# Spreading the root of three RMS norms over the partitions: two transfers through DRAM in place of four products

## The chip, the cores and the metric

The kernel runs on one core of one Trainium2 chip. A core has five engines that work side by side, each through its own queue in its own order: TensorE (PE in the profile; its weight loads are PEld), VectorE (DVE), ScalarE (ACT), GpSimd (POOL) and SyncE (SP), which here only issues transfers (DMAs). The engines share the on-chip memory SBUF (128 partitions); TensorE writes its results to PSUM, which GpSimd does not use here. The metric is the time of one execution on the device in microseconds; lower is better.

## What is computed

One encoder layer, then a final norm, for 1024 prompt tokens and 256 sample tokens of width 1024 with the same weights:

```python
def rmsnorm(x, w):
    y = xf * lax.rsqrt(jnp.mean(xf * xf, -1, keepdims=True) + EPS)
    return (y * w.astype(jnp.float32)).astype(x.dtype)
...
x = x + merged @ w_out
x = x + memory_cross_attention(rmsnorm(x, norm_xa_w), rmsnorm(mem, norm_mem_w), xa_w_q, xa_w_kv, xa_w_o)
h = rmsnorm(x, norm_ffn_w)
gu = h @ ffn_w_gate_up
x = x + (jax.nn.silu(gu[..., :D_FF]) * gu[..., D_FF:]) @ ffn_w_down
...
return rmsnorm(x, final_norm_w)
```

All of it is float32. The change touches the norm before the feed-forward part (`norm_ffn_w`) and the final norm, both for some of the tokens only.

## The kernel before

Activations lie feature-major: a tile is 128 features on the partitions by the tokens along the free axis, and the width of 1024 is eight such tiles (`KT`, index k). Tokens go in three blocks (`BLOCKS`): 0 and 1 are 512 prompt tokens each, 2 is the 256 sample tokens. Every float32 product is done as three products of split operands: a matrix is copied to a high half (`hi`, `whi`, on ScalarE) and the rest is subtracted into a low half (`lo`, `wlo`, on VectorE or GpSimd); `mm3` multiplies hi by hi, hi by lo and lo by hi into one PSUM bank (a tile of 128x512, `bank`). L108 is the line of nearly every product, L125 and L126 are those of the two splits.

The mean square of a token is a sum over features, so over partitions. `Norm.add` squares each of the eight tiles on ScalarE and adds them up in `acc` (named nacc in the profile) on VectorE or GpSimd. `Norm.rest` then does, in this order:

- Products of 128 tokens of `acc` by a column of ones (128x1), one for each of the `nb` = 4 groups of 128 tokens: the sums lie with tokens on the partitions, 128x4.
- On that small tile, `rsqrt` on VectorE (L231 to L235): `y` (nst in the profile), the reciprocal root of the mean square, 128x4.
- The way back to features on the partitions: four products of a column of `y`, broadcast, by the identity. They leave in one bank the root of each of 512 tokens, the same on all partitions.
- Eight multiplications by that root and the weight column, one for each k. Most are one scalar_tensor_tensor on VectorE (L294), which reads the tile from SBUF and the root from the bank. For the k in `shared`, ScalarE multiplies by the weight column ahead of time (L289) and GpSimd by the root (L290), which it reads from a copy in SBUF that ScalarE makes from the bank (L286, into `acc`).
- `sink(k, t)` hands each result on.

Three uses matter here. I call them the first, the second and the third place:

- The first is the feed-forward norm of block 0, in `OutProj.run`: all eight k on VectorE, in place; the sink splits the results into the feed-forward input. It runs while TensorE does the output projection of blocks 1 and 2. Ahead of it SyncE stores the block before the norm to DRAM (`x2d`).
- The second is the final norm of block 1, in `last_norm`, started after phase 5 (of 0 to 6) of the prompt's down projection. k = 1, 3, 5 and 7 are GpSimd's. The sink stores each result to the output `yT`: odd k from SyncE's queue, even k from ScalarE's.
- The third is the final norm of block 0, started after phase 6, so it runs beside the sample's down projection (`down_sample`). k = 1, 4 and 6 are GpSimd's. In `down_sample` each of 22 rows of weights for each half of the width is split by `prep` into one of four buffer pairs (`his`, `los`) while TensorE works on the earlier ones; `prep(n + 4)` follows tile n.

Beside the second and third place the sample's activations come back from DRAM: SyncE loads `graw`, ScalarE and VectorE split it into gs (`g_room`). At the end of phase 6 VectorE evacuates four banks of sums into x (L2241); the sample's down projection uses these banks next.

The order of the work: the body is a main generator with side generators. A planner's clock counts the nominal time of TensorE's products, and a side generator goes on when the clock reaches the time that it last asked for with `yield`. So `lag`, `lag2` and `pace` (in ns of that clock) set where a norm's steps stand in program order. TensorE keeps that order; for the other engines a scheduler orders instructions by what they depend on. Waits are semaphores; an engine that waits holds up what is behind it in its queue.

Of the kernel before, what the change touches and what calls it, by code (L numbers as in the profile page):

```python
# [8 lines left out]
F32 = mybir.dt.float32  # L9
F32R = mybir.dt.float32r  # L10
I32 = mybir.dt.int32
AF = mybir.ActivationFunctionType
ALU = mybir.AluOpType
# [4 lines left out]
P = 128  # L18
D = 1024
KT = D // P  # L20
# [147 lines left out]
def trunk_kernel(ctx: ExitStack, tc: tile.TileContext, a):  # L168
    nc = tc.nc
    V, S, G, T, SY = nc.vector, nc.scalar, nc.gpsimd, nc.tensor, nc.sync  # L170
    K = Trunk(ctx, tc, a)
# [19 lines left out]
    n = 0  # L191
# [25 lines left out]
    ident = cst[:, C_ID : C_ID + P]  # L217
# [6 lines left out]
    def bank(p=pq, tag="b"):  # L224
        return p.tile([P, 512], F32, tag=tag, name="bank")
# [11 lines left out]
    class Norm:  # L237
# [21 lines left out]
                (eng or V).tensor_tensor(out=self.acc, in0=self.acc, in1=sq, op=ALU.add)  # L259
            self.k += 1  # L260

        def rest(self, xk, wcol, sink, pace=1300, shared=(), lag=1500, ks=range(KT), inplace=False, ready=None, halves=1, lag2=2800, rooms=()):

            p, n = self.p, self.n
            nb = n // P
            yield lag
            pc = bank()
            parts = [self.acc[:, i * n : (i + 1) * n] for i in range(halves)]
            if self.apart is not None:
                parts.append(self.apart)  # L270
            for c in range(nb):
                for t in parts:
                    mm(pc[:, c : c + 1], t[:, c * P : (c + 1) * P], one, t is parts[0], t is parts[-1])
            y = p.tile([P, 4 if p is xp else 16], F32, tag="nst", name="nst", bufs=2)[:, :nb]
            ms, sc = pc[:, 4 : 4 + nb], pc[:, 8 : 8 + nb]
            V.tensor_scalar(out=ms, in0=pc[:, :nb], scalar1=1.0 / D, scalar2=EPS, op0=ALU.mult, op1=ALU.add)
            rsqrt(y, ms, sc)
            yield lag2
            pb = bank()
            for c in range(nb):  # L280
                mm(pb[:, c * P : (c + 1) * P], y[:, c : c + 1].to_broadcast([P, P]), ident)
            while ready is not None and not ready():
                yield 300
            if shared:
                rb = self.acc
                S.activation(rb, pb[:, :n], AF.Copy)  # L286
            for k in ks:
                if k in shared:
                    S.activation(xk(k), xk(k), AF.Copy, scale=sm[:, wcol + k : wcol + k + 1])  # L289
                    G.tensor_tensor(out=xk(k), in0=xk(k), in1=rb, op=ALU.mult)  # L290
                    sink(k, xk(k))
                    continue
                t = bank() if k in rooms else xk(k) if shared or inplace else p.tile([P, 512], F32, tag="nsq", name="nt", bufs=self.sq)[:, :n]
                V.scalar_tensor_tensor(out=t, in0=xk(k), scalar=sm[:, wcol + k : wcol + k + 1], in1=pb[:, :n], op0=ALU.mult, op1=ALU.mult)  # L294
                sink(k, t)
                yield pace * n / 512

    def rstd_of(nm, y, lag, lag2=0, halves=1):
        n = nm.n
        nb = n // P  # L300
        yield lag
        pc = bank()
        parts = [nm.acc[:, i * n : (i + 1) * n] for i in range(halves)]
        for c in range(nb):
            for t in parts:
                mm(pc[:, c : c + 1], t[:, c * P : (c + 1) * P], one, t is parts[0], t is parts[-1])
        ms, sc = pc[:, 4 : 4 + nb], pc[:, 8 : 8 + nb]
        V.tensor_scalar(out=ms, in0=pc[:, :nb], scalar1=1.0 / D, scalar2=EPS, op0=ALU.mult, op1=ALU.add)
        rsqrt(y, ms, sc)
        yield lag2  # L310

    def norm(p, xk, n, wcol, sink, pace=1300, step=700, lag=1500):
        nm = Norm(p, n)
# [1131 lines left out]
    class OutProj:  # L1445
# [21 lines left out]
        def run(self, xsrc, scale, wcol, xpool, store, sinks=None, then=None, after=None):  # L1467


            ps = (xpool,) * 3 if sinks is None else (x0p, xhp, xpool)  # L1470
            x = [p.tile([P, KT, n], F32, tag=f"x{b}", name=f"x{b}") for b, (p, (_, n)) in enumerate(zip(ps, BLOCKS))]
            for ks in (slice(0, 2), slice(2, 8)):
                for b, (t0, n) in enumerate(BLOCKS):
                    SY.dma_start(x[b][:, ks, :], xsrc[:, ks, t0 : t0 + n])
            nms = [Norm(xpool, n) for _, n in BLOCKS]

            def evac(m, b, ps):
                V.scalar_tensor_tensor(out=x[b][:, m, :], in0=ps, scalar=scale, in1=x[b][:, m, :], op0=ALU.mult, op1=ALU.add)
                nms[b].add(x[b][:, m, :])

            begun, self.first = self.first, []
            for i, (m, b) in enumerate((m, b) for m in range(2) for b in range(3)):
                if i < len(begun):
                    yield from proj(begun[i], self.ws[m], self.src, b, range(KT - 2, KT))
                    evac(m, b, begun[i])
                else:
                    yield from self.parts(m, b, range(KT))
                    evac(m, b, self.first[-1])
                if (m, b) == (1, 0):
                    K.ahead()  # L1490
            hs = self.hs
            for b, (t0, n) in enumerate(BLOCKS):
                for m in range(2, KT):
                    if b == 0:
                        self.ws.append(K.take())
                    ps = bank(pm)[:, :n]
                    yield from proj(ps, self.ws[m], self.src, b)
                    if b == 0 and m < KT - 1 or b == 2 and m == 6:
                        K.ahead()
                    evac(m, b, ps)  # L1500
                    if b == 2 and after is not None:
                        after(m)
                if b == 0:
                    hs += act_tiles()
                if then is not None and b == 0:
                    then()
                if store is not None:
                    SY.dma_start(store[:, :, t0 : t0 + n], x[b])
                xk = lambda k, b=b: x[b][:, k, :]
                if sinks is None:  # L1510
                    norm_b = nms[b].rest(xk, wcol, to_h(hs, b), 600)
                else:
                    norm_b = nms[b].rest(xk, wcol, sinks(b, hs), PACES[b], ks=range(KT) if b != 1 else SECOND_KS, inplace=True, lag2=LAGS2[b])
                K.pending[id(hs), b] = K.side(norm_b)
            self.x = x

# [759 lines left out]
    def last_norm(nm, b):  # L2276
        t0, n = BLOCKS[b]

        def sink(k, t):
            (SY if k % 2 else S).dma_start(a["yT"][:, k, t0 : t0 + n], t)  # L2280

        if b < 2:
            K.side(nm.rest(lambda k: x2[b][:, k, :], S_FIN, sink, PACEF, SHARED[b], LAGF[b], lag2=LAGF2[b]))
            return
        pb = bank()
        ms, y = pb[:, :n], pb[:, n : 2 * n]
        parts = [nm.acc, *nm.apart]
        for t in parts:
            mm(ms, mean.to_broadcast([P, P]), t, t is nm.acc, t is parts[-1])
        r = x2p.tile([P, 512], F32, tag="nacc", name="seed", bufs=2)[:, :n]  # L2290
        S.activation(r, ms, AF.Abs_reciprocal_sqrt, bias=eps)
        V.scalar_tensor_tensor(out=y, in0=ms, scalar=EPS, in1=r, op0=ALU.add, op1=ALU.mult)
        V.scalar_tensor_tensor(out=y, in0=y, scalar=-0.5, in1=r, op0=ALU.mult, op1=ALU.mult)
        xk = lambda k: x2[b][:, k, :]
        for k in EARLY_K:
            G.tensor_tensor(out=xk(k), in0=xk(k), in1=r, op=ALU.mult)
        root = bank()[:, :n]
        for k in EARLY_K:
            V.scalar_tensor_tensor(out=xk(k), in0=y, scalar=1.5, in1=xk(k), op0=ALU.add, op1=ALU.mult)
            sink(k, xk(k))  # L2300
            if k == EARLY_K[0]:
                V.scalar_tensor_tensor(out=root, in0=y, scalar=1.5, in1=r, op0=ALU.add, op1=ALU.mult)
                S.activation(nm.acc, root, AF.Copy)
                for j in (2, 0):
                    G.tensor_tensor(out=xk(j), in0=xk(j), in1=nm.acc, op=ALU.mult)
        for k in (4, 2, 5, 6, 0, 7):
            if k > 3:
                V.scalar_tensor_tensor(out=xk(k), in0=xk(k), scalar=sm[:, S_FIN + k : S_FIN + k + 1], in1=root, op0=ALU.mult, op1=ALU.mult)
            sink(k, xk(k))
# [95 lines left out]
MIX = 6500  # L2405
A1, A2, A3, A4 = 1200, 800, 2000, 600
DEC, CONV = 1200, 600
FIRST_W, PACES, LAGS2 = 9000, (600, 1300, 600), (2800, 9500, 9500)
LAGX = (26000, 17000, 9000)
FIRST_V = (1, 3, 5, 6, 7)  # L2410
LAG0, LAGF, LAGF2, PACEF = 9700, (8000, 6000, 1500), (9000, 9000, 2800), 1000

SHARED, EARLY_K = ((1, 4, 6), (1, 3, 5, 7)), (1, 3)

# [78 lines left out]
```

## Time and profile before

| | |
|---|---|
| median of 3 runs | 2184.68 us (2183.58 to 2186.11) |
| profiled execution | 2185.21 us |
| its span, first to last instruction | 2183.4 us |
| granted TensorE clock, mean | 0.998 of full speed |
| the root's products on TensorE, all norms | 60 records of 128x128, 275 ns median |
| ScalarE's copies of the root (L286) | 2, 598 ns |
| GpSimd's multiplications by the root (L290) | 7, 1291 ns median |
| VectorE's multiplications by the root (L294), 128x512 | 467 to 749 ns over all shapes |
| transfers | 253.04 MB, mean 116 GB/s |

The span is divided by engine and line; a wait is given as the engine and line that waited, what it waited for, the total, the number of times and the longest. In a timeline a row is one instruction or a run of equal ones: start, duration, engine, line, operation, tile written and tiles read, shapes, count, and in brackets the idle time ahead of it and what ended it. TensorE's matmuls overlap, so their starts tell the pace. DMA rows give the size and the time from issue to landing.

### The profile page before, as it was taken

How to read it: one execution, taken by the hardware profiler on the slowest of the kernel's cores; microseconds unless marked ns; L12 is line 12 of the kernel's file. 1: busy time of each engine (PE TensorE's matmuls, PEld its weight loads, DVE VectorE, ACT ScalarE, POOL GpSimd, SP SyncE). 2: the span in 40 equal slices, each digit the busy share in tenths (PEclk: the TensorE clock that was granted, in tenths of full speed). 3: DMA queues.
4: the chain of work that ended last, by engine and by line, in shares of the span. 5: the costliest groups of instructions: out<-in, count | busy, mean ns of one | idle time of the engine just before them, and what ended most of it. 6: DMA issues, size and time to landing. Idle time of an engine off the chain costs nothing.

```text
span 2183.4 us, 31946 instructions
## 1 busy us (share of the span) xinstructions
PE 2169.1 (99%) x12184; PEld 1888.5 (86%) x12184; DVE 1354.3 (62%) x2615; ACT 885.7 (41%) x1651; POOL 592.8 (27%) x399
## 2 busy tenths in 40 slices
PE   9999999999999999999999999999999999999998
PEld 8988888888888888888988888888888888888888
DVE  7868678786874846677644556544434444478575
ACT  6433263544535553125544523332322323343454
POOL 2010110101001010052412432566666665200031
PEclk9999999999999999999999999999999999999999
DMA  5221423323244546631522421322222222493531
GB/s 195 92 93 54 113 61 95 84 66 93 76 121 123 169 134 225 203 131 55 178 73 108 158 97 63 104 86 84 83 77 80 84 98 90 147 348 119 205 112 59
DMA packets 194297, 253.04 MB, mean 116 GB/s; under 512 B 76933, under 2 KB 109269, under 8 KB 194143
## 3 DMA queue, kind: packets, MB, share of 16 engines
q1 hardware_dynamic: 177886, 227.14, 31.8%
q10 hardware_dynamic: 16256, 23.86, 3.0%
q8 instruction: 95, 1.56, 0.3%
q14 instruction: 60, 0.48, 0.1%
HBM read 178.02 MB, written 72.94 MB: 115 GB/s over the span
## 4 chain that ended last, share of the span: by engine, by line
PE 94%; DVE 3%; DMA 1%; ACT 1%; issue 0%; SPq 0%; POOL 0%; DVEq 0%; ACTq 0%; POOLq 0%
PE bank L108 93%; PE bank L121 1%; DMA braw<-gq 1%; DMA raw<-in_w_sv 0%; DVE gb L819 0%; DVE nt L294 0%; DVE U L948 0%; ACT junk L517 0%; DVE aT L814 0%; DMA gb<-grd 0%; DVE lo L126 0%; DVE bank L294 0%; DMA uc<-usd 0%; DVE gt L491 0%; DVE nacc L259 0%
## 5 line engine op out<-in xcount | busy, mean ns | idle before, releaser
L108 PE MATMUL bank<-hi,whi 128*128 128x512 f32 (+1 forms) x1976 | 700.9, 355 | 0.2 <-DVE vg L493 0.2
L108 PE MATMUL bank<-lo,whi 128*128 128x512 f32 (+1 forms) x1976 | 687.7, 348 | 0.0
L108 PE MATMUL bank<-hi,wlo 128*128 128x512 f32 (+1 forms) x1976 | 687.4, 348 | 0.0
L108 PEld LDWEIGHTS bank<-hi,wlo 128*128 128x128 f32 x1976 | 374.3, 189 | 47.9
L108 PEld LDWEIGHTS bank<-hi,whi 128*128 128x128 f32 x1976 | 375.0, 190 | 45.8 <-issue 1.4
L108 PEld LDWEIGHTS bank<-lo,whi 128*128 128x128 f32 x1976 | 375.1, 190 | 43.2
L125 ACT ACTIVATE whi<-raw 128x1024 fp32r<-128x1024 f32 (+1 forms) x136 | 137.0, 1009 | 249.5 <-PE bank L108 221.5
L126 POOL TENSOR_TENSOR wlo<-raw,whi 128x1024 fp32r<-128x1024 f32 x65 | 158.1, 2433 | 293.9 <-ACT whi L125 293.9
L126 DVE TENSOR_TENSOR wlo<-raw,whi 128x1024 fp32r<-128x1024 f32 (+1 forms) x71 | 80.8, 1140 | 74.6 <-ACT whi L125 74.4
L108 PE MATMUL bank<-bhl,whi 128*128 128x512 f32 x408 | 125.9, 390 | 0.0
L126 POOL TENSOR_TENSOR wlo<-x,whi 128x1024 fp32r<-128x1024 f32 x40 | 96.6, 2414 | 47.5 <-ACT whi L125 47.5
L2123 DVE TENSOR_TENSOR x<-x,bank 128x512 f32<-128x512 f32 x21 | 14.5, 689 | 124.5 <-ACT x L1918 124.5
L108 PEld LDWEIGHTS bank<-bhl,whi 128*128 128x128 f32 x408 | 76.4, 188 | 16.4 <-ACT whi L125 0.4
L697 DVE SCALAR_TENSOR_TENSOR acc<-craw,sm,acc 128x510 f32<-128x510 f32 (+1 forms) x96 | 73.2, 762 | 24.6 <-ACT acc L695 22.8
L1931 DVE SCALAR_TENSOR_TENSOR t<-t,x 128x512 f32<-128x512 f32 x42 | 63.9, 1521 | 28.7 <-ACT t L1930 28.7
L125 ACT ACTIVATE whi<-x 128x1024 fp32r<-128x1024 f32 (+1 forms) x48 | 49.2, 1025 | 77.5 <-PE bank L108 69.6
L108 PE MATMUL bank<-bhl,wlo 128*128 128x512 f32 x204 | 79.6, 390 | 0.5 <-DVE wlo L126 0.5
L1940 DVE SCALAR_TENSOR_TENSOR t<-bank,t 128x512 f32<-128x512 f32 (+1 forms) x44 | 24.5, 557 | 81.4 <-PE bank L108 81.4
L108 PE MATMUL bank<-bhl,ahl 128*128 128x512 f32 x312 | 75.0, 395 | 0.0
L1069 ACT ACTIVATE gs<-bank 128x512 f32<-128x512 f32 (+1 forms) x60 | 31.2, 520 | 101.2 <-PE bank L108 94.2
L1918 ACT ACTIVATE x<-bank 128x512 f32<-128x512 f32 x63 | 37.6, 597 | 82.0 <-PE bank L108 79.3
L108 PEld LDWEIGHTS bank<-bhl,ahl 128*128 128x128 f32 x312 | 58.8, 189 | 13.6
(420 smaller groups left out, 4459.1 us busy)
## 6 DMA issues: line engine op xcount, KB each, us to landing
raw<-in_w_gu SPq DMA_DIRECT2D x44, 512.0 KB, 3.4
braw<-gq SPq DMA_DIRECT2D x14, 1024.0 KB, 7.5
raw<-in_w_g SPq DMA_DIRECT2D x20, 512.0 KB, 3.3
gq<-t SPq DMA_DIRECT2D x33, 256.0 KB, 2.1
gtd<-gs ACTq DMA_DIRECT2D x32, 256.0 KB, 2.2
w<-in_w_dn SPq DMA_DIRECT2D x8, 1024.0 KB, 9.7
raw<-in_w_qkv SPq DMA_DIRECT2D x12, 512.0 KB, 3.6
gq<-r SPq DMA_DIRECT2D x22, 256.0 KB, 2.0
```

Source lines behind the costliest of these rows:

```text
L108: self.nc.tensor.matmul(out, l, r, start=start, stop=stop, skip_group_check=more)
L121: self.nc.tensor.transpose(out, x, ident)
L125: self.last_hi = self.nc.scalar.activation(hi, src, AF.Copy).ins
L126: (eng or self.nc.vector).tensor_tensor(out=lo, in0=src, in1=f32(hi), op=ALU.subtract)
L697: V.scalar_tensor_tensor(out=dst, in0=src, scalar=wj, in1=dst, op0=ALU.mult, op1=ALU.add)
L1069: S.activation(t, ps, AF.Tanh, scale=0.5)
L1918: S.activation(t, ps, AF.Copy)
L1931: V.scalar_tensor_tensor(out=t, in0=t, scalar=1.0, in1=src, op0=ALU.add, op1=ALU.mult)
L1940: V.scalar_tensor_tensor(out=out, in0=u, scalar=sign, in1=t, op0=ALU.mult, op1=ALU.mult)
L2123: V.tensor_tensor(out=c22, in0=c22, in1=pe, op=ALU.add)
```

## The change

In the three places the root no longer goes through TensorE. SyncE writes `y` to a row of a small DRAM tensor, `rows_d` (three rows of 512 floats): each partition writes its four values, 16 bytes, so that token 128 c + p stands at position 4 p + c. A second transfer reads that row, broadcast to all 128 partitions, into `acc`. All multiplications then take the root from `acc` in SBUF, through a view with steps of four elements (16 bytes) that puts the tokens back in order. The copies by ScalarE go. Other norms keep the products.

The planner's lags change too: between the root and the read stand 3500 (`ROW`), after it `lag2`, 7000 at the first place (2800 before) and 6500 at the other two (9000 before).

```diff
-        def rest(self, ..., halves=1, lag2=2800, rooms=()):
+        def rest(self, ..., halves=1, lag2=2800, rooms=(), row=None):
...
             rsqrt(y, ms, sc)
-            yield lag2
-            pb = bank()
-            for c in range(nb):
-                mm(pb[:, c * P : (c + 1) * P], y[:, c : c + 1].to_broadcast([P, P]), ident)
+            if row is not None:
+                SY.dma_start(row.rearrange("(p c) -> p c", c=nb), y)
+                yield ROW
+                SY.dma_start(self.acc, row.unsqueeze(0).to_broadcast([P, n]))
+                yield lag2
+                rb = pb = self.acc.rearrange("q (p c) -> q c p", c=nb)
+            else:
+                yield lag2
+                pb = bank()[:, :n]
+                for c in range(nb):
+                    mm(pb[:, c * P : (c + 1) * P], y[:, c : c + 1].to_broadcast([P, P]), ident)
+                if shared:
+                    rb = self.acc
+                    S.activation(rb, pb, AF.Copy)
             while ready is not None and not ready():
                 yield 300
-            if shared:
-                rb = self.acc
-                S.activation(rb, pb[:, :n], AF.Copy)
+            like = (lambda x: x) if row is None else quad
             for k in ks:
                 if k in shared:
                     S.activation(xk(k), xk(k), AF.Copy, scale=sm[:, wcol + k : wcol + k + 1])
-                    G.tensor_tensor(out=xk(k), in0=xk(k), in1=rb, op=ALU.mult)
+                    G.tensor_tensor(out=like(xk(k)), in0=like(xk(k)), in1=rb, op=ALU.mult)
...
-                V.scalar_tensor_tensor(out=t, in0=xk(k), ..., in1=pb[:, :n], op0=ALU.mult, op1=ALU.mult)
+                V.scalar_tensor_tensor(out=like(t), in0=like(xk(k)), ..., in1=pb, op0=ALU.mult, op1=ALU.mult)
...
+    rows_d = dp.tile([3, 512], F32, name="rows_d")
...
-    ... inplace=True, lag2=LAGS2[b])
+    ... inplace=True, lag2=LAGS2[b], row=rows_d[2] if b == 0 else None)
...
-            K.side(nm.rest(..., LAGF[b], lag2=LAGF2[b]))
+            K.side(nm.rest(..., LAGF[b], lag2=LAGF2[b], row=rows_d[b]))
...
-... LAGS2 = ..., (2800, 9500, 9500)
+... LAGS2 = ..., (7000, 9500, 9500)
...
-LAG0, LAGF, LAGF2, PACEF = 9700, (8000, 6000, 1500), (9000, 9000, 2800), 1000
+LAG0, LAGF, LAGF2, PACEF = 9700, (8000, 6000), (6500, 6500), 1000
+ROW = 3500
```

TensorE's order loses the twelve products and is otherwise the same. In the changed kernel the lines behind L262 are some ten higher: L2241 becomes L2251, L2280 L2290, L2320 L2330, L294 L302 and L290 L298. What moves on the other engines is shown at two places (tiles carry buffer numbers, which differ between the two programs).

At the second place, SyncE's queue in the change; nst is the root, nacc its copy on all partitions, graw a load for the sample's splits, yT the output, x1 the block's tiles:

```order
L2330 DMA graw_18628<-gsd_12372 128x256 x2
L279 DMA rows_d_79<-nst_18484 128x4
L2330 DMA graw_18633<-gsd_12372 128x256 x2
L281 DMA nacc_17277<-rows_d_79 128x512
L2330 DMA graw_18638<-gsd_12372 128x256 x2
L2290 DMA yT<-x1_17274 128x512 x4
L2330 DMA graw_18643<-gsd_12372 128x256 x2
```

The write (L279) and the read (L281) stand with one load between them and one behind, ahead of the four outputs; the rest of this piece is as before.

VectorE at the second place, before (gs and wlo are low halves, x0 evacuations of the last phase):

```order
L294 SCALAR_TENSOR_TENSOR x1_17276<-x1_17276,sm_78,bank_18566 128x512 x4
L126 TENSOR_TENSOR wlo_18718<-raw_17327,whi_18717 128x512
L126 TENSOR_TENSOR gs_18633<-graw_18634,gs_18633 128x512
L126 TENSOR_TENSOR gs_18633<-graw_18639,gs_18633 128x512
L126 TENSOR_TENSOR gs_18633<-graw_18644,gs_18633 128x512
L126 TENSOR_TENSOR wlo_18718<-w1_17273,whi_18717 128x512
L2241 SCALAR_TENSOR_TENSOR x0_17275<-bank_17281,x0_17275 128x512
L2241 SCALAR_TENSOR_TENSOR x0_17275<-bank_17282,x0_17275 128x512
L126 TENSOR_TENSOR gs_18633<-graw_18649,gs_18633 128x512
L2241 SCALAR_TENSOR_TENSOR x0_17275<-bank_17283,x0_17275 128x512
```

And in the change:

```order
L302 SCALAR_TENSOR_TENSOR x1_17274<-x1_17274,sm_78,nacc_17277 128x512 x4
L126 TENSOR_TENSOR gs_18627<-graw_18628,gs_18627 128x512
L126 TENSOR_TENSOR gs_18627<-graw_18633,gs_18627 128x512
L126 TENSOR_TENSOR gs_18627<-graw_18638,gs_18627 128x512
L126 TENSOR_TENSOR wlo_18712<-raw_17325,whi_18711 128x512
L126 TENSOR_TENSOR wlo_18712<-w1_17271,whi_18711 128x512
L2251 SCALAR_TENSOR_TENSOR x0_17273<-bank_17279,x0_17273 128x512
L126 TENSOR_TENSOR gs_18627<-graw_18643,gs_18627 128x512
L2251 SCALAR_TENSOR_TENSOR x0_17273<-bank_17280,x0_17273 128x512
L2251 SCALAR_TENSOR_TENSOR x0_17273<-bank_17281,x0_17273 128x512
```

The four multiplications now read nacc, not a bank; the first weight split moved behind the three activation splits, and the fourth activation split (its load is the one behind SyncE's four outputs) stands ahead of the second evacuation. ScalarE's halves of these splits follow its four outputs of even k in the same order.

VectorE at the third place, before (hi1, w0 and lo1 are weights in SBUF, x0 the block's tiles):

```order
L126 TENSOR_TENSOR wlo_18720<-w0_17272,whi_18719 128x512 x2
L126 TENSOR_TENSOR wlo_18718<-hi1_17270,whi_18717 128x512
L294 SCALAR_TENSOR_TENSOR x0_17275<-x0_17275,sm_78,bank_18945 128x512
L126 TENSOR_TENSOR wlo_18718<-hi1_17270,whi_18717 128x512
L294 SCALAR_TENSOR_TENSOR x0_17275<-x0_17275,sm_78,bank_18945 128x512 x2
L126 TENSOR_TENSOR wlo_18720<-hi1_17270,whi_18719 128x512
```

And in the change:

```order
L126 TENSOR_TENSOR wlo_18714<-w0_17270,whi_18713 128x512 x2
L302 SCALAR_TENSOR_TENSOR x0_17273<-x0_17273,sm_78,nacc_17278 128x512 x2
L126 TENSOR_TENSOR wlo_18712<-hi1_17268,whi_18711 128x512
L302 SCALAR_TENSOR_TENSOR x0_17273<-x0_17273,sm_78,nacc_17278 128x512 x2
L126 TENSOR_TENSOR wlo_18712<-hi1_17268,whi_18711 128x512
L302 SCALAR_TENSOR_TENSOR x0_17273<-x0_17273,sm_78,nacc_17278 128x512
```

The multiplications begin one split earlier in the order, with two of them ahead of the first hi1 split instead of none. On ScalarE the first two outputs now stand behind that tile's high half and ahead of the next one's; the first of them is k = 4, a product of GpSimd's.

More of the change, by code (lines that the diff above doesn't have):

```diff
@@ L260, in add, with rest @@
             self.k += 1
-        def rest(self, xk, wcol, sink, pace=1300, shared=(), lag=1500, ks=range(KT), inplace=False, ready=None, halves=1, lag2=2800, rooms=()):
+        def rest(self, xk, wcol, sink, pace=1300, shared=(), lag=1500, ks=range(KT), inplace=False, ready=None, halves=1, lag2=2800, rooms=(), row=None):
             p, n = self.p, self.n
@@ L293, in rest @@
                 t = bank() if k in rooms else xk(k) if shared or inplace else p.tile([P, 512], F32, tag="nsq", name="nt", bufs=self.sq)[:, :n]
-                V.scalar_tensor_tensor(out=t, in0=xk(k), scalar=sm[:, wcol + k : wcol + k + 1], in1=pb[:, :n], op0=ALU.mult, op1=ALU.mult)
+                V.scalar_tensor_tensor(out=like(t), in0=like(xk(k)), scalar=sm[:, wcol + k : wcol + k + 1], in1=pb, op0=ALU.mult, op1=ALU.mult)
                 sink(k, t)
@@ L1512, in run @@
                 else:
-                    norm_b = nms[b].rest(xk, wcol, sinks(b, hs), PACES[b], ks=range(KT) if b != 1 else SECOND_KS, inplace=True, lag2=LAGS2[b])
+                    norm_b = nms[b].rest(xk, wcol, sinks(b, hs), PACES[b], ks=range(KT) if b != 1 else SECOND_KS, inplace=True, lag2=LAGS2[b], row=rows_d[2] if b == 0 else None)
                 K.pending[id(hs), b] = K.side(norm_b)
@@ L2282, in last_norm @@
         if b < 2:
-            K.side(nm.rest(lambda k: x2[b][:, k, :], S_FIN, sink, PACEF, SHARED[b], LAGF[b], lag2=LAGF2[b]))
+            K.side(nm.rest(lambda k: x2[b][:, k, :], S_FIN, sink, PACEF, SHARED[b], LAGF[b], lag2=LAGF2[b], row=rows_d[b]))
             return
@@ L2407 @@
 DEC, CONV = 1200, 600
-FIRST_W, PACES, LAGS2 = 9000, (600, 1300, 600), (2800, 9500, 9500)
+FIRST_W, PACES, LAGS2 = 9000, (600, 1300, 600), (7000, 9500, 9500)
 LAGX = (26000, 17000, 9000)
 FIRST_V = (1, 3, 5, 6, 7)
-LAG0, LAGF, LAGF2, PACEF = 9700, (8000, 6000, 1500), (9000, 9000, 2800), 1000
+LAG0, LAGF, LAGF2, PACEF = 9700, (8000, 6000), (6500, 6500), 1000
+ROW = 3500
 SHARED, EARLY_K = ((1, 4, 6), (1, 3, 5, 7)), (1, 3)
```

## The prediction

> **What bounds the kernel now.** I read the busy shares first, then the chain that ended last, then TensorE's waits.
>
> ```profile
> PE 2169.1 (99%) x12184; PEld 1888.5 (86%) x12184; DVE 1354.3 (62%) x2615; ACT 885.7 (41%) x1651; POOL 592.8 (27%) x399
> PE 94%; DVE 3%; DMA 1%; ACT 1%; issue 0%; SPq 0%; POOL 0%; DVEq 0%; ACTq 0%; POOLq 0%
> PE bank L108 <- DVE vg L493: 1.1, 2, 0.9
> ...
> PE bank L108 <- DVE U L948: 0.2, 1, 0.2
> ```
>
> TensorE (PE) is busy 99% of the span, 94% of the last chain is its own, and the nine groups of its waits run from 1.1 us down to 0.2. So a product taken out of its queue is worth its full time, and everything else in the change is worth nothing until it makes TensorE wait. The sum therefore has two sides: what TensorE no longer does, and the first new waits.
>
> **What is removed.** The root's four products stand three times in TensorE's timeline (columns: start, duration, engine, line, tiles, shape, count; a 128x128 f32 product makes two records):
>
> ```profile
> 1296.31 1.05 PE L108 MATMUL bank<-cst,nst 128*128 128x128 f32 x8
> 1297.12 0.48 PE L108 MATMUL bank<-hi,whi 128*128 128x512 f32 x1
> 1297.43 0.39 PE L108 MATMUL bank<-lo,whi 128*128 128x512 f32 x1
> 1297.66 0.39 PE L108 MATMUL bank<-hi,wlo 128*128 128x512 f32 x1
> ...
> 2094.85 1.05 PE L108 MATMUL bank<-cst,nst 128*128 128x128 f32 x8
> 2095.66 0.71 PE L108 MATMUL bank<-bhl,whi 128*128 128x512 f32 x2
> ...
> 2107.91 0.39 PE L108 MATMUL bank<-bhl,wlo 128*128 128x512 f32 x1
> 2108.14 0.40 PE L108 MATMUL bank<-gs,whi 128*128 128x256 f32 x2
> ...
> 2108.49 0.40 PE L108 MATMUL bank<-gs,whi 128*128 128x256 f32 x2
> ...
> 2128.81 1.05 PE L108 MATMUL bank<-cst,nst 128*128 128x128 f32 x8
> 2129.62 0.48 PE L108 MATMUL bank<-gs,whi 128*128 128x256 f32 x2
> ```
>
> Matmuls overlap, so starts count, not durations. At the first place the eight records take 1297.12 - 1296.31 = 0.81 us of starts, and the product behind them holds 0.31 us where the one after it holds 0.23: 0.89 us. The other two places also show 0.81 (2095.66 - 2094.85, 2129.62 - 2128.81), and I give them the same 0.08 of recovery. **Gain: 3 x 0.89 = 2.7 us.** The two copies of the root on ScalarE (L286) go too, off the path.
>
> **What is added: a root that comes by two transfers.** SyncE's queue gets a 2 KB write in pieces of 16 bytes, which waits for the root, and a 256 KB broadcast read, which waits for the write. No row has exactly these; the nearest bound them (KB each, median us from issue to landing):
>
> ```profile
> xsd<-gb SPq DMA_DIRECT2D x40, 32.0 KB, 1.7
> usd<-UT SPq DMA_DIRECT2D x20, 64.0 KB, 3.9
> ga<-gtd SPq DMA_DIRECT2D x16, 256.0 KB, 2.6
> gb<-grd SPq DMA_DIRECT2D x10, 512.0 KB, 4.0
> ```
>
> Write: 1.7 (256 pieces) to 3.9 (1024 pieces of 64 bytes). With 128 pieces it is nearer the first: 1.7. Read: 2.6 (same size) to 4.0 (a broadcast, twice the size). I take 2.6. With 0.3 us for two issues the root lands 4.6 us after its last VectorE step, 8.2 at the upper ends.
>
> *First place* (feed-forward norm of block 0):
>
> ```profile
> 1290.15 35.03 SPq L1508 DMA_DIRECT2D x2d<-x  x2
> x2d<-x SPq DMA_DIRECT2D x2, 2048.0 KB, 8.6
> ...
> 1343.14 0.40 PE L108 MATMUL bank<-hi,whi 128*128 128x512 f32 x1
> 1305.95 1.67 POOL L126 TENSOR_TENSOR lo<-x,hi 128x512 fp32r<-128x512 f32 x1 [0.91 <-ACT hi L125]
> ```
>
> The write may queue behind the 2 MB store issued at 1290.15, which takes 8.6 us, so the root may land as late as 1303. VectorE's multiplications stand at their place in its order some microseconds later. The cover is the output projection of blocks 1 and 2: TensorE first reads the finished block at 1343.1, and its last piece is ready today at 1305.95 + 1.67 = 1307.6. Even 12 us later leaves 23. On SyncE's queue only the next 2 MB store stands behind the read, due near 1325 (two issues span 35.03 us). Cost: nothing.
>
> *Second place* (final norm of block 1). These are VectorE's and GpSimd's rows today:
>
> ```profile
> 2090.36 0.15 DVE L235 SCALAR_TENSOR_TENSOR nst<-bank,nst 128x4 f32<-128x4 f32 x1
> ...
> 2096.63 2.73 DVE L294 SCALAR_TENSOR_TENSOR x<-x,sm,bank 128x512 f32<-128x512 f32 x4 [2.71 <-ACT nacc L286]
> 2099.27 1.75 DVE L126 TENSOR_TENSOR wlo<-raw,whi 128x512 fp32r<-128x512 f32 x1
> ...
> 2108.33 0.69 DVE L2241 SCALAR_TENSOR_TENSOR x<-bank,x 128x512 f32<-128x512 f32 x1 [0.67 <-PE bank L108]
> 2096.67 5.51 POOL L290 TENSOR_TENSOR x<-x,nacc 128x512 f32<-128x512 f32 x4 [14.66 <-ACT nacc L286]
> L1940 DVE SCALAR_TENSOR_TENSOR x<-x,t x21: 683/1666/1667, 1398.9 to 1900.2; 128x512 f32<-128x512 f32 x21
> ```
>
> The root is ready at 2090.5, so it lands at 2095.1, before the 2096.6 of today. But the multiplications change kind. Today they read the root from PSUM and run at 0.68 us each beside GpSimd, while the next instruction, with both inputs in SBUF, takes 1.75 beside it. L1940 shows the two prices for a scalar_tensor_tensor with both inputs in SBUF: 683 ns, and 1666 in most of its runs. Now all four read the root from SBUF, as GpSimd's four do. I count 0.7 + 3 x 1.67 = 5.7 us: done at 2100.8, where today it is 2099.4. ScalarE then issues the four outputs and starts the splits held behind them; VectorE follows at 2101.9 with five split steps at about 0.61 each (to 2104.9), an evacuation, another split (its load waits on SyncE behind GpSimd's outputs), and three evacuations. TensorE's first product after that stage moves from 2108.14 to 2107.24 and needs the four evacuated banks at 2107.24, 2107.60, 2107.96 and 2108.32 (0.36 a group, 2108.14 to 2108.49). By this count the four are done at about 2105.3, 2106.6, 2107.2 and 2108.1. All in time, the second by 1.0 us, the others by less. Between 0 and 0.5 us is lost if the first multiplication is blocked too; I take 0.2.
>
> *Third place* (final norm of block 0, during the sample's down projection). Here every weight tile is split just ahead of TensorE, ScalarE's half (hi) and then VectorE's (lo), one tile in 2127.81 - 2126.37 = 1.44 us:
>
> ```profile
> 2126.37 0.63 ACT L125 ACTIVATE whi<-w 128x512 fp32r<-128x512 f32 x1 [0.81 <-PE bank L108]
> 2127.81 0.63 ACT L125 ACTIVATE whi<-hi 128x512 fp32r<-128x512 f32 x1 [0.81 <-PE bank L108]
> ...
> 2122.28 0.16 DVE L235 SCALAR_TENSOR_TENSOR nst<-bank,nst 128x4 f32<-128x4 f32 x1
> ...
> 2127.04 0.69 DVE L126 TENSOR_TENSOR wlo<-w,whi 128x512 fp32r<-128x512 f32 x1 [0.75 <-ACT whi L125]
> 2128.48 0.69 DVE L126 TENSOR_TENSOR wlo<-hi,whi 128x512 fp32r<-128x512 f32 x1 [0.75 <-ACT whi L125]
> 2130.64 4.25 POOL L290 TENSOR_TENSOR x<-x,nacc 128x512 f32<-128x512 f32 x3 [17.78 <-ACT nacc L286]
> ```
>
> A split begins when TensorE leaves a tile and fills the buffers of the fourth tile after it. For the one at 2127.81 three tiles lie between, and the low half is first read 0.24 us into its tile: 2127.75 + 3 x 1.44 + 0.24 = 2132.3, with the root products gone. VectorE's half ends today at 2129.2: 3.1 us of slack. Now two multiplications stand ahead of it and two more ahead of the next. The root is ready at 2122.4 and lands at 2127.0; the multiplications may start at 2127.7. Beside GpSimd's three they run in rounds of 1.67-1.75: 2128.9, 2130.6, then the split, also blocked, at 2132.3: just in time. Two more multiplications (0.65 each, GpSimd done) and the next split end at 2134.3, needed at 2133.7. **Lost: about 0.5 us.** ScalarE's next split waits here behind an output of GpSimd's second product, until about 2130.8; that is inside the same slack.
>
> **Sum.** The profiled execution took 2185.2 us, its span 2183.4 and 1.8 around it. -2.7 + 0 + 0.2 + 0.5 = -2.0, so 2183.2 for it; it lay 0.5 over the median of 2184.68, so **2182.7** for the median.
>
> **One price this rests on.** GpSimd and VectorE now read the root in steps of 16 bytes. The rows with steps:
>
> ```profile
> L837 DVE COPY UT<-W x5: 1120/1122/1123, 229.9 to 735.1; 64x1024 f32<-64x1024 f32 x5
> L841 ACT ACTIVATE W<-W x5: 1094/1099/1102, 234.0 to 739.9; 128x512 f32<-128x512 f32 x5
> L1930 ACT ACTIVATE t<-x x42: 611/616/633, 1382.3 to 1894.7; 128x512 f32<-128x512 f32 x42
> L290 POOL TENSOR_TENSOR x<-x,nacc x7: 1282/1291/1746, 2096.7 to 2133.6; 128x512 f32<-128x512 f32 x7
> ```
>
> VectorE reads a transposed tile (L837, steps of 128 bytes) at 1.1 ns an element, the rate of its contiguous rows (0.69 us for 512): nothing added there. At ScalarE's ratio, below, a multiplication would take 0.5 more, some 2 us of stall in all, inside the range. ScalarE pays 1099 against 616 ns for steps of 64 bytes. GpSimd has no such row: 1.29 us (L290, contiguous) to 1.29 x 1099/616 = 2.30. The step is the smallest of the three and GpSimd's own row is the nearest in operation, so I take 1.29.
>
> **Rivals.**
> *GpSimd pays for the steps.* Each of its products d longer. At the second place its fourth output comes 4d later, and the split on SyncE's load behind it holds the second evacuation; with 1.0 us of slack TensorE loses 4d - 1.0. At the third place three rounds stand ahead of the first split: 3d + 0.5. Together 7d - 0.5 against 2.7: from d = 0.46 (1.75 us a product) the change loses. At ScalarE's ratio d is 1.0 and the sum -2.7 + 6.5 = +3.8: 2188.5. For it: the only other engine without a shared row pays; against: VectorE's L837. The Trainium skill, "GPSIMD Engine Reference", section 7 on pitfalls, says that reading SBUF in steps over 8 bytes costs GpSimd about half as much again; no row here shows it, and by that figure, an estimate of 1.94 us a product, the time would be 2186.0.
> *The transfers land late.* At 3.9 and 4.0 us the root lands 3.6 later. Then VectorE stands with splits and evacuations queued behind its first multiplication: second place 3.6 less the least slack of 0.8, 2.8 us; third 2130.6 + 0.7 + 2 x 1.67 = 2134.6 against 2132.3, and 0.4 behind it, 2.7. -2.7 + 5.5 = +2.8: 2187.5. Against: the small-piece rows reach this only with 64 KB.
> *All hidden.* No new wait at all: -2.7, 2182.0.
> *It frees nothing*, because the tensor queue meets the same weights later anyway: 2184.7. Against: no such wait among the nine.
>
> **How the numbers follow.** Forecast 0.45, all hidden 0.12, GpSimd's steps 0.25, late landing 0.12, nothing 0.06. The range goes from all hidden with 0.3 off for scatter, 2181.7, to the dearest steps, 2188.5. A measurement of this kernel tells 0.2% (4.4 us) from no change: faster would be under 2180.3, beyond the whole gain, 0.03; slower over 2189.1, which takes dear steps and a late root together, 0.08; the same 0.89.
>
> **What would show it.** TensorE's timeline without nst records, and three times 0.9 us gone. VectorE's L302 rows: 0.7 to 1.7 us. GpSimd's L298 rows near 1.3 to 1.75 us if I am right, near 2 or above for the steps. The two transfers' landing, 1.7 and 2.6. TensorE's waits: new ones on x L2251 at 2107 and on wlo L126 at 2133, under 1 us together. A wait on nacc beyond 2096 or 2128 on VectorE means the late landing; waits over 3 us together would make the prediction wrong.

## The result and the profile after

The changed kernel takes 2193.07 us (median of 6 runs, 2192.22 to 2194.8), the one before 2184.5 in the same session (2183.58 to 2186.11): 1.004 times as long, 95% interval 1.003 to 1.0051. The forecast was 2182.7 and its range ended at 2188.5, so both were wrong. The profiled execution took 2192.36 us, its span 2190.6.

The busy shares and the chain that ended last, of the kernel after:

```profile
PE 2169.9 (99%) x12160; PEld 1888.0 (86%) x12160; DVE 1368.1 (62%) x2615; ACT 884.7 (40%) x1649; POOL 599.4 (27%) x399
PE 92%; DVE 4%; DMA 1%; ACT 1%; issue 1%; POOL 0%; SPq 0%; DVEq 0%; ACTq 0%; POOLq 0%
```

The 24 matmul records are gone (12184 to 12160). TensorE's (PE) own share of the chain falls from 94% to 92%, and VectorE's (DVE) grows. TensorE's waits (total, times, longest) say where; the first line is before's, the other two are after's:

```profile
PE bank L108 <- DVE wlo L126: 0.5, 1, 0.5
...
PE bank L108 <- DVE wlo L126: 3.8, 3, 2.3
PE bank L108 <- DVE x L2251: 3.7, 2, 2.7
```

L2251 (L2241 before) is the evacuation at the second place, and before there was no wait on it. The 0.5 us on a split's low half (wlo) stands near 1907 to 1909 in both kernels, far from the three places. So 7.0 us of waits are new: 3.7 at the second place, 3.3 at the third. The multiplications behind them, after (count, then least, median and longest ns):

```profile
L302 DVE SCALAR_TENSOR_TENSOR x<-x,sm,nacc x17: 1119/1172/2474, 1300.9 to 2140.2; 128x512 f32<-128x512 f32 x17
L298 POOL TENSOR_TENSOR x<-x,nacc x7: 2004/2402/2480, 2095.0 to 2135.7; 128x512 f32<-128x512 f32 x7
2094.92 8.16 DVE L302 SCALAR_TENSOR_TENSOR x<-x,sm,nacc 128x512 f32<-128x512 f32 x4 [2.87 <-DMA nacc<-rows_d]
2130.75 3.56 DVE L302 SCALAR_TENSOR_TENSOR x<-x,sm,nacc 128x512 f32<-128x512 f32 x2
2134.24 2.04 DVE L126 TENSOR_TENSOR wlo<-hi,whi 128x512 fp32r<-128x512 f32 x1
2136.20 3.47 DVE L302 SCALAR_TENSOR_TENSOR x<-x,sm,nacc 128x512 f32<-128x512 f32 x2
```

Without GpSimd (POOL) beside it a multiplication takes 1.12 to 1.17 us, and beside it up to 2.47. GpSimd's go from 1.29 to 2.0-2.5. At the second place four take 8.16 us where the forecast counted 5.7, and at the third even the split between them takes 2.04.

TensorE's timeline and its granted clock (PEclk, the column before the last two), after, show a second loss:

```profile
2108.22 0.47 PE L108 MATMUL bank<-gs,whi 128*128 128x256 f32 x2 [2.67 <-DVE x L2251]
...
2109.81 0.80 PE L108 MATMUL bank<-gs,whi 128*128 128x256 f32 x2 [1.01 <-DVE x L2251]
...
2110.62 0.63 PE L108 MATMUL bank<-gs,whi 128*128 128x256 f32 x2
...
2111.26 0.63 PE L108 MATMUL bank<-gs,whi 128*128 128x256 f32 x2
...
2140.33 0.50 PE L108 MATMUL bank<-gs,wlo 128*128 128x256 f32 x1 [2.31 <-DVE wlo L126]
2109.50:2113.00 3.50, 3.19 (x15) 3.19 (x16) 2.88 (x5) 3.41 (x7) 3.16 (x3) 0.53 0.52 176
2140.30:2143.80 3.50, 3.47 (x16) 3.47 (x17) 3.41 (x5) 0.63 (x1) 0.00 (x0) 0.52 0.39 150
2143.80:2148.00 4.20, 4.20 (x37) 4.20 (x36) 2.08 (x5) 1.47 (x3) 0.00 (x0) 0.99 0.01 2
```

At each of the two places the clock is halved for 3.3 to 3.4 us (0.53 and 0.52 over 3.5). A group of three products then takes 2111.26 - 2110.62 = 0.64 us instead of 0.36, for five groups: 5 x 0.28 = 1.4 us at each place. Such a stretch is counted as busy PE time, so the wait view does not show it.

The account: the profiled execution of after was already 1.2 us ahead of before's at 1061 us, in front of the first place. Single profiles differ there by -1.8 to +0.4 us, so differences under 1 us are read from medians, or from rows on both sides of a place, not from spans. The span grew 7.2, so 8.4 us are to be explained. Waits +7.0, slow clock +2.8 and products -2.7 (1.0 is seen at the first place) make 7.1, 1.3 short. TensorE's rows show that about 1.0 of it lies in the same two stages. From the last bhl product ahead of the second place's stage (2107.91 before, 2105.16 after) to the first product on nacc behind it (2117.49 and 2120.37) the change loses 5.6 us. From there to the first product of the last norm (2173.65 and 2180.85) it loses 4.3, or 5.2 with its products' 0.9 taken out. What makes up that 1.0 beside the listed waits and the slow clock is open.

### The profile page after: what moved, and what is told of

The parts are those of the page before. It is cut to its first block, busy times and chain, and to the rows that moved or that the text cites. A ratio compares the mean times of both kernels' runs of the same rounds, so it can differ in the third digit from the quotient of the medians.

```text
span 2190.6 us, 31904 instructions
## 1 busy us (share of the span) xinstructions
PE 2169.9 (99%) x12160; PEld 1888.0 (86%) x12160; DVE 1368.1 (62%) x2615; ACT 884.7 (40%) x1649; POOL 599.4 (27%) x399
## 4 chain that ended last, share of the span: by engine, by line
PE 92%; DVE 4%; DMA 1%; ACT 1%; issue 1%; POOL 0%; SPq 0%; DVEq 0%; ACTq 0%; POOLq 0%
PE bank L108 91%; PE bank L121 1%; DMA braw<-gq 1%; DVE x L302 0%; DVE bhl L126 0%; DVE gb L829 0%; PE bank L404 0%; DVE nt L302 0%; DVE wlo L126 0%; DVE U L958 0%; DMA nacc<-rows_d 0%; ACT junk L527 0%; DVE aT L824 0%; DMA gb<-grd 0%; DVE lo L126 0%
```

## The experiments

Theories: **1**, the 16-byte steps in which both engines read the root; **2**, that VectorE and GpSimd now both read SBUF alone, steps or not; **3**, the root's late landing; and for the slow clock, that it follows from the waits.

**Places apart: the first, the second, the third alone.** The other places keep their products and their lags of before.

```diff
# first alone
-    ..., lag2=LAGF2[b], row=rows_d[b]))
+    ..., lag2=LAGF2[b]))
...
# second alone (third alone: rows_d[0] if b == 0)
-    ..., lag2=LAGS2[b], row=rows_d[2] if b == 0 else None)
+    ..., lag2=LAGS2[b])
-    ..., lag2=LAGF2[b], row=rows_d[b]))
+    ..., lag2=LAGF2[b], row=rows_d[1] if b == 1 else None))
```

> The changed kernel with transfers and steps at the first place alone (feed-forward norm of block 0); the two final norms have the four products and the copy of before. If the products' time at TensorE is a full gain where nothing waits, 0.9 us less than before: 2183.5 to 2183.9, no wait of TensorE on x or wlo beyond those of before, VectorE's multiplications there at 1.1 to 1.2 us, hidden. Rival: the freed time is waited away behind the same weights: 2184.4 to 2184.8.

> Transfers and steps at the second place alone (final norm of block 1). If the loss there is its own: TensorE waits about 3.7 us on the evacuations, then runs at about half the granted clock for some 3 us (1.4 us lost), against 0.9 gained: 2188 to 2189.2. Rival (the slower clock behind the wait costs nothing, since TensorE would have waited later): 2187 to 2187.6. Rival (the wait is only pushed on into the stage of the third place and absorbed there): 2184 to 2185.5.

> Transfers and steps at the third place alone (final norm of block 0, beside the sample's down projection). If the loss there is its own: about 3.5 us of waits on the low halves (wlo), then half the clock for some 3 us (1.4 us), against 0.9 gained: 2188 to 2189.2. Rival (the third place is late only because the second one is): waits under 1 us, 2183.6 to 2185.

Measured, against 2184.49: first alone 2182.97 (ratio 0.9998, 0.9989 to 1.0007), second alone 2189.13 (1.0023, 1.0014 to 1.0032), third alone 2190.1 (1.0024, 1.0013 to 1.0035). That is -1.5, +4.6 and +5.6, together +8.7 against 8.6 of the whole change: the two final norms are the loss, each on its own. The second fell into its bracket. That the three add up so closely is in part luck. The first came out 0.5 below its bracket, and its interval holds 1, so by time alone it can't be told from before. Its rows show the gain: from the first product on nacc at this place to the first one behind it TensorE takes 52.95 us (1290.20 to 1343.15) where it took 53.93 (1291.96 to 1345.89), with no new wait. So the products gave 1.0 where 0.9 was counted. The third came out 0.9 above its bracket: alone, its slow clock lasted 6.7 us, twice as long as in the changed kernel (its row stands in the part on the clock).

**Token order.** The write scatters the root into token order, so that nobody reads in steps.

```diff
-                SY.dma_start(row.rearrange("(p c) -> p c", c=nb), y)
+                SY.dma_start(row.rearrange("(c p) -> p c", p=P), y)
-                rb = pb = self.acc.rearrange("q (p c) -> q c p", c=nb)
+                rb = pb = self.acc
...
```

> The changed kernel, but the write puts the root into DRAM in token order (512 pieces of 4 bytes), so both engines read it in SBUF without steps; all three places keep their transfers and have no products. Theory 1 (the 16-byte steps are the price): VectorE's multiplications fall to 0.69 us alone and 1.67 beside GpSimd, GpSimd's from 2.0-2.4 to 1.29-1.75, TensorE's new waits of 3.8 and 3.7 us shrink to 1.5 us together and the slow clock behind them goes: 2182 to 2184. Theory 2 (the price is that VectorE and GpSimd now both read only SBUF, with steps or without): VectorE stays at 2.0 to 2.5 beside GpSimd, the waits stay within 1 us of 7.5 together: 2191 to 2193. Theory 3 (the root lands about 1 us later than forecast and that is what is late): the multiplications get shorter, but about 1 us is lost at each of the two places: 2184.5 to 2186.5.

2210.32 us (1.0117, 1.0103 to 1.0131): all three theories missed it. The write's own row and its landing, then TensorE's waits and GpSimd's products, of this kernel:

```profile
L279 SPq DMA_DIRECT2D rows_d<-nst x3: 370/371/383, 1294.0 to 2136.3; - x3
DMA to landing us min/median/max: 9.8/9.8/9.8
PE bank L108 <- DVE x L2251: 8.4, 2, 8.0
PE bank L108 <- DVE wlo L126: 8.1, 2, 7.5
L298 POOL TENSOR_TENSOR x<-x,nacc x7: 1704/1715/1804, 2108.7 to 2153.2; 128x512 f32<-128x512 f32 x7
```

512 pieces of 4 bytes land after 9.8 us, the change's 128 pieces of 16 bytes after 1.4. The root comes so late that the run cannot judge the steps by its time; GpSimd's products do fall to 1.71.

**The engines' price without any transfer.** Both of these are the kernel before, with products; only where the root is read in the two final norms differs.

```diff
# VectorE from ScalarE's plain copy in SBUF
-                V.scalar_tensor_tensor(..., in1=pb[:, :n], ...)
+                V.scalar_tensor_tensor(..., in1=rb if shared else pb[:, :n], ...)
# and, for the second, ScalarE's copy interleaved
-                S.activation(rb, pb[:, :n], AF.Copy)
+                rb = self.acc.rearrange("q (p c) -> q c p", c=nb)
+                S.activation(rb, quad(pb[:, :n]), AF.Copy)
...
```

> The kernel before, products and copy kept, no transfers; only VectorE's multiplications in the two final norms take the root from ScalarE's copy in SBUF, without steps, in place of the bank. This is what the prediction counted for those places: VectorE 0.7 then 1.67 beside GpSimd, GpSimd 1.29 to 1.75. If the count was right: under 0.7 us of new waits, 2184.5 to 2185.4. Rival (two engines that read only SBUF are dear even without steps): waits of 1 to 2 us at each place and the slow clock behind them: 2188 to 2190.

> The kernel before, products and copy kept, no transfers; in the two final norms ScalarE writes its copy interleaved, and both engines read the root in steps of 16 bytes. Theory 1 (the steps are most of the loss): VectorE 2.0 to 2.5 us beside GpSimd and 1.1 to 1.2 alone, GpSimd 2.0 to 2.4; waits of 2 to 3 us and the slow clock at each place: 2189 to 2193. Theory 3 (the transfers' late landing is most of it): waits of 1 us or less at each place: 2184.5 to 2187.

Without steps 2187.45 against 2184.67 (1.0014, 1.0005 to 1.0023), between the two brackets; with steps 2194.61 (1.0049, 1.0036 to 1.0061), 1.6 above theory 1's. VectorE's and GpSimd's groups and TensorE's waits, first without, then with steps, there with ScalarE's copy:

```profile
L294 DVE SCALAR_TENSOR_TENSOR x<-x,sm,nacc x9: 739/1777/1889, 2097.6 to 2141.2; 128x512 f32<-128x512 f32 x9
L290 POOL TENSOR_TENSOR x<-x,nacc x7: 1289/1733/1743, 2097.6 to 2136.4; 128x512 f32<-128x512 f32 x7
PE bank L108 <- DVE wlo L126: 1.5, 2, 1.0
PE bank L108 <- DVE x L2241: 0.9, 1, 0.9
```
```profile
L296 DVE SCALAR_TENSOR_TENSOR x<-x,sm,nacc x9: 1131/2421/2555, 2097.0 to 2146.9; 128x512 f32<-128x512 f32 x9
L292 POOL TENSOR_TENSOR x<-x,nacc x7: 1549/2392/2418, 2097.0 to 2140.7; 128x512 f32<-128x512 f32 x7
PE bank L108 <- DVE wlo L126: 4.2, 4, 2.3
PE bank L108 <- DVE x L2243: 3.8, 2, 2.8
L287 ACT ACTIVATE nacc<-bank x2: 1084/1102/1120, 2095.9 to 2135.7; 128x512 f32<-128x512 f32 x2
```

So the loss stands without a single transfer. In TensorE's rows, between the same products as above (2107.78, 2123.18 and 2184.73 in this run), the run with steps loses 5.8 us at the second place and 5.4 at the third, where the changed kernel loses 5.6 and 5.2. By the medians, reading SBUF on both engines costs 2.8 us (theory 2, part of it; 1.1 to 5.0 by its interval) and the steps 7.2 more (theory 1). Not all of the 7.2 is the two engines' own: ScalarE's copy takes 1.10 us instead of 0.60, so each place starts 0.5 us later, and the longer waits bring two stretches of half clock, 2.8 us together, which the profile without steps does not have. The medians of the two engines are alike in each run, 1.78 and 1.73, then 2.42 and 2.39, as when they take turns: a round holds one product of each and is 0.3 us shorter than the two alone (0.74 + 1.29, then 1.13 + 1.55). The steps add to a round what they add to each engine: VectorE alone goes from 0.74 to 1.13 (+0.39), GpSimd's least from 1.29 to 1.55 (+0.26), and the round from 1.73 to 2.39 (+0.66). The Trainium skill, "SBUF — State Buffer", "SBUF: two separate sides", says that VectorE with two SBUF inputs and GpSimd reading SBUF hold one port pair in turn for a whole instruction; these equal medians agree.

**One engine out of the way.** The changed kernel, but ScalarE copies the landed root in token order: into a bank for VectorE alone; or into plain SBUF for both; or into a bank for VectorE and from there into plain SBUF for GpSimd.

```diff
# VectorE from the bank, GpSimd in steps
+                if shared:
+                    pb = bank()[:, :n]
+                    S.activation(quad(pb), rb, AF.Copy)
...
# both from plain SBUF
+                if shared:
+                    rb = p.tile([P, 512], F32, tag="nsq", name="nroot", bufs=self.sq)[:, :n]
+                    S.activation(quad(rb), pb, AF.Copy)
+                    pb = rb
...
# bank and plain: the first, and behind it
+                    rb = p.tile([P, 512], F32, tag="nsq", name="nroot", bufs=self.sq)[:, :n]
+                    S.activation(rb, pb, AF.Copy)
...
```

> The changed kernel, but in the two final norms ScalarE copies the landed root once, in token order, into a PSUM bank for VectorE; GpSimd still reads it in steps from SBUF. VectorE back at 0.7 us each. If the two engines' sharing is what makes GpSimd dear, it falls to 1.29 to 1.75: 2182.3 to 2184. If the steps are GpSimd's own price it stays at 2.0 or more, its outputs hold the loads on SyncE's queue at the second place and the splits at the third: 2186 to 2189.

> The changed kernel with its 16-byte write and broadcast read, but in the two final norms ScalarE first copies the landed root into token order in SBUF (one copy of 0.65 to 1.1 us, behind the landing), and both engines read that copy without steps. Theory 1 (steps): VectorE 1.46 to 1.8 and GpSimd 1.7 as in the token-order run, waits of 1.5 to 3 us together: 2183.5 to 2186.5. Theory 2 (both reading SBUF is the price): VectorE 2 and more, 2190 to 2193.

> As the run in which ScalarE copies the landed root into a bank for VectorE, and ScalarE then copies the bank into SBUF in token order for GpSimd (0.6 us more, ahead of its first product), so that nothing but ScalarE's first copy reads in steps. If the steps are GpSimd's remaining price (1.53 to 1.57 us beside a VectorE that reads the bank): its products fall to 1.29 us, its fourth output comes about 0.5 us sooner, 2181.8 to 2182.9. Rival (the root's arrival decides, and the second copy is as dear as the steps): 2182.5 to 2184.

VectorE from the bank: 2182.76 against 2184.67 (0.9993, 0.9984 to 1.0002). ScalarE's copy, GpSimd's and VectorE's groups (the last with the feed-forward norms that also read banks) and two of TensorE's waits (the one on wlo is again the one near 1907):

```profile
L286 ACT ACTIVATE bank<-nacc x2: 1093/1112/1131, 2095.2 to 2127.4; 128x512 f32<-128x512 f32 x2
L303 POOL TENSOR_TENSOR x<-x,nacc x7: 1532/1567/2035, 2095.3 to 2130.5; 128x512 f32<-128x512 f32 x7
L307 DVE SCALAR_TENSOR_TENSOR x<-x,sm,bank x25: 467/737/750, 1337.9 to 2134.3; 128x512 f32<-128x512 f32 x17, 128x256 f32<-128x256 f32 x8
PE bank L108 <- DVE wlo L126: 0.5, 1, 0.5
PE bank L108 <- DVE x L2256: 0.5, 1, 0.5
```

The transfers and GpSimd's steps are all still there, and the loss of 8.6 us is gone: it needed VectorE reading the root from SBUF. GpSimd's steps alone cost it 0.27 us a product, and that hides. By the medians this run gains 1.9 us, not 2.7, and its interval holds 1. TensorE's rows show where gain is lost, at the second place: against before it is 1.3 us ahead at the first product on nacc there (2082.42), 2.2 at the last bhl product (2105.72), with the norm's products gone, and 0.9 at the next product on nacc (2116.61). So the place gives its 0.9 back and some 0.4 more. The root's landing and ScalarE's copy behind it come together there; no run parts them.

Both from plain SBUF: 2190.12 (1.0027, 1.0015 to 1.0038). By its time this is theory 2's, by its rows not: VectorE takes 1.78 at the median, as without transfers, and not 2 or more. But the copy (1.13 us) comes on top of the landing, and TensorE waits 4.0 on x and 2.9 on wlo. Bank and plain: 2188.77 against 2184.17 (1.0022, 1.0013 to 1.0031); missed by both sides. GpSimd is at 1.30 us, but the second copy changed the order of issue: six loads now stand on SyncE behind GpSimd's outputs, where two stood in the run before, and ScalarE sits idle for one. SyncE's row, ScalarE's row and TensorE's wait, of this kernel:

```profile
2103.03 2.78 SPq L2337 DMA_DIRECT2D graw<-gsd  x6
2105.88 0.63 ACT L125 ACTIVATE gs<-graw 128x512 fp32r<-128x512 f32 x1 [5.68 <-DMA graw<-gsd]
PE bank L108 <- DVE x L2258: 2.6, 3, 1.6
```

This says nothing of the engines' prices; it shows how thin the second place's cover is.

**Is there a version that beats both?** From the run with VectorE on the bank: norms begun 1.5 us earlier; or the second place left on products.

```diff
# earlier
-LAG0, LAGF, LAGF2, PACEF = 9700, (8000, 6000), (6500, 6500), 1000
+LAG0, LAGF, LAGF2, PACEF = 9700, (6500, 4500), (6500, 6500), 1000
# first and third
-    ..., lag2=LAGF2[b], row=rows_d[b]))
+    ..., lag2=LAGF2[b], row=rows_d[0] if b == 0 else None))
-LAG0, LAGF, LAGF2, PACEF = 9700, (8000, 6000), (6500, 6500), 1000
+LAG0, LAGF, LAGF2, PACEF = 9700, (8000, 6000), (6500, 9000), 1000
```

> As the run in which ScalarE copies the landed root into a bank for VectorE, with both final norms begun 1.5 us earlier in the issue order (lags 6500 and 4500 in place of 8000 and 6000). What is left of the loss there is 0.9 us at the second place, behind GpSimd's fourth output, the load that SyncE issues behind it and the split. If the root's late landing is its cause, it goes: 2181.3 to 2182.3. Rival (the squares' sum is not ready sooner, or the moved splits are late instead): 2182.5 to 2184.

> Transfers at the first and third place, the third with ScalarE's copy into a bank for VectorE; the second place keeps its products. If the copy takes VectorE out of GpSimd's way at the third place too, no wait over those of before and two sets of products gained: 2182.6 to 2183.3. Rival (the third place loses by the landing what its products gave): 2183.5 to 2184.2.

Against 2184.17: earlier 2184.0 (0.9998, 0.9989 to 1.0007), first and third 2182.69 (0.9994, 0.9985 to 1.0003). The earlier start came out in its rival's bracket. It removes the wait on x, but TensorE's first groups at the second place then start 0.60 us apart instead of 0.36, and at the third it waits 0.25 and 0.22 on the splits. The groups follow VectorE's four evacuations, which in this run stand in one row behind a split whose load came late:

```profile
2104.81 2.48 DVE L2256 SCALAR_TENSOR_TENSOR x<-bank,x 128x512 f32<-128x512 f32 x4
```

First and third fell into its bracket. These versions beat the changed kernel by 9 to 10 us; none can be told from the kernel before, since each interval holds 1.

**The clock behind a wait.** The kernel before, with VectorE's low half of two weight tiles repeated, after all norms.

```diff
-        (eng or self.nc.vector).tensor_tensor(out=lo, in0=src, in1=f32(hi), op=ALU.subtract)
+        self.splits = getattr(self, "splits", 0) + 1
+        for _ in range(1 + EXTRA.get(self.splits, 0)):
+            (eng or self.nc.vector).tensor_tensor(out=lo, in0=src, in1=f32(hi), op=ALU.subtract)
...
+EXTRA = {456 - 12: 7, 456 - 4: 10}
```

> The kernel before, nothing of its computation or of its norms changed; in the sample's down projection, after the last norm, VectorE repeats the low half of one weight tile 7 times near 2151 and that of another 10 times near 2162.5 (each repeat 0.61 us, the slack there about 3.1), so TensorE waits on wlo once for about 1 to 1.5 us and once for about 3 us, away from all that the change touches. Theory (the slow clock follows from the length of the wait alone): 1.00 granted behind the short wait, about 0.5 for some 3.5 us behind the long one, which costs 1.4 us more than the waits: 2189.5 to 2191. Rival (the slow clock belongs to the norms' stages, not to the waits): 1.00 behind both, 2188 to 2189.2.

2196.88 against 2184.73 (1.0055, 1.0039 to 1.0072). Other splits slipped in between the repeats, so both waits came out longer than meant, 3.3 and 5.5 us, and the time lies above both brackets. The short wait that was to leave the clock alone was not reached. TensorE's timeline, three stretches behind the first wait and one behind the second:

```profile
2157.91 0.39 PE L108 MATMUL bank<-gs,wlo 128*128 128x256 f32 x1 [3.29 <-DVE wlo L128]
...
2176.64 0.58 PE L108 MATMUL bank<-gs,wlo 128*128 128x256 f32 x1 [5.47 <-DVE wlo L128]
2157.90:2159.70 1.80, 1.78 (x13) 1.79 (x14) 0.00 (x0) 0.36 (x1) 0.00 (x0) 0.91 0.00 0
2159.70:2162.90 3.20, 3.20 (x18) 3.20 (x17) 1.21 (x2) 0.90 (x2) 0.00 (x0) 0.52 0.02 5
2162.90:2166.90 4.00, 4.00 (x36) 4.00 (x35) 1.57 (x3) 1.63 (x3) 0.00 (x0) 1.00 0.00 0
...
2176.40:2179.90 3.50, 3.26 (x15) 3.26 (x16) 0.41 (x2) 0.63 (x1) 0.00 (x0) 0.51 0.00 0
```

The clock halves behind both, with no norm or GpSimd near and hardly a transfer (the DMA share is 0.02 and 0.00): it follows from the wait. 8.8 us of new waits and 2 x 1.4 of slow clock make 11.6 of the 12.2 lost. For short waits the other runs speak. Behind single waits of 0.93 and 0.99 us, in the run without transfers and steps, the clock stays full:

```profile
2110.00:2114.00 4.00, 3.07 (x24) 2.81 (x24) 2.83 (x5) 3.86 (x8) 3.62 (x3) 1.00 0.64 220
2139.00:2143.00 4.00, 3.00 (x25) 2.95 (x25) 4.00 (x7) 2.43 (x5) 0.00 (x0) 1.00 0.88 340
```

With the third place alone, waits of 1.52 and 1.77 us within 4 us were enough, and the clock stayed at half for 6.7 us, twice as long as behind each wait just shown:

```profile
2134.55 0.50 PE L108 MATMUL bank<-gs,whi 128*128 128x256 f32 x2 [1.52 <-ACT whi L125]
2136.82 0.58 PE L108 MATMUL bank<-gs,wlo 128*128 128x256 f32 x1 [1.77 <-DVE wlo L126]
2135.70:2142.40 6.70, 5.58 (x26) 5.58 (x27) 4.66 (x8) 2.41 (x4) 0.00 (x0) 0.50 0.41 160
```

## Why the prediction was wrong, step by step

- **What bounds the kernel**: right. TensorE's queue sets the time; the first place alone shows its products as 1.0 us gained (0.89 counted) and nothing late, as it was costed ("Cost: nothing").
- **The failing step: "nothing added" for VectorE's steps.** It was read from L837, a copy with one input, and set beside 0.69 us for 512, a row with two. L837's 1.1 ns an element is indeed what one input takes without steps (L522, 542 ns for 512 in the kernel before), but the multiplication has two inputs in SBUF, and its 0.74 us became 1.13 alone. Why two inputs pay and one does not, no run shows. The prediction allowed for "0.5 more, some 2 us of stall in all"; but beside GpSimd every round also carries GpSimd's 0.26, blocked splits included, so a round went from 1.73 to 2.39. The runs put the steps at 7.2 us, the slow clock behind them and up to 1 us for ScalarE's stepped copy included.
- **The count at the second and third place without steps** (0.2 and 0.5) was too small as well. The run nearest to it, which keeps products and copy, lost 2.8. VectorE took 1.78, not 1.67, and the first multiplication of the four, counted at 0.7, was blocked too (1.88), so the four took 7.0 us where 5.7 was counted. Slacks of tenths of a microsecond could not hide that.
- **The slow clock** stood in no term: 1.4 us at each place, two fifths of what the waits cost.
- **The landing**: the write took 1.4 us (1.7 taken), the read 3.8 (2.6 taken). At the second place the root was multiplied 6.3 us after its last step instead of 4.6, at the third 5.4 as counted (5.3). It is not the loss: with the same transfers and VectorE out of the way the time is 2182.76, not over the kernel before. It may be why the second place gains nothing even then, but ScalarE's copy stands there too.
- **The rival that GpSimd pays** had the sign and the right place, but the wrong engine as cause. Its break-even of 1.75 us a product was not reached: 1.55 to 1.57 with VectorE out of the way. The rest of its 2.0 to 2.5 in the changed kernel goes when VectorE leaves SBUF. So the sign set for this rival, "near 2 or above", came up without it being the cause. The Trainium skill, "GPSIMD Engine Reference", section 7, says half as much again for reading SBUF in steps over 8 bytes; here it was 1.57 against 1.29, a fifth.
- **The range** took the dearest steps (2188.5) as its end, for one engine and without the clock, and so ended 4.6 us short. The chance of 0.08 for slower by over 0.2% was far too low: VectorE's and GpSimd's price for the steps, taken to be alternatives, come together in one round.

## What to carry to other kernels

Where two engines take turns at SBUF, as here, the price of a slower access is paid by both in every round, and by whatever is queued behind them. Look for an input that can come from PSUM before counting steps: here one ScalarE copy of 1.1 us took away the whole loss. An operation's price under a new access pattern is read from a row with the same number of inputs. Where waits of TensorE add up to some three microseconds within five, count the slow stretch too.

## What the runs showed of the hardware

- The granted clock fell to half for about 3.4 us at TensorE waits of 3.29 and 5.47 us alone, and at waits of 2.3 to 2.8 us with one of about 1 us close by (some 1.4 us lost each time). At 1.52 and 1.77 us close together it stayed at half for 6.7 us. It stayed full behind single waits of 0.93 and 0.99 us and, with both engines on plain SBUF, behind 1.09 and 1.26 us some 3 us apart. After the wait of 3.29 us it began some 1.5 us after work had resumed. The Trainium skill, "TensorE: Matmul & The Clock Gate", Part 1, names half rate and about 3.4 us of work to leave it, which agrees; it gives an idle window of about 3.4 us as what starts it, where 2.67 and 1.01 us close together sufficed here.
- Reading SBUF in steps of 16 bytes: VectorE's two-input multiplication 0.74 to 1.13 us, ScalarE's copy 1.11 against 0.60 us from a bank without steps, GpSimd's product 1.29 to 1.55.
- 2 KB written to DRAM lands after 1.4 us in 128 pieces of 16 bytes and after 9.8 us in 512 pieces of 4 bytes.
